# Re-placing the fixed order of sums, splits and hidden work in a seven-product matmul pipeline, and giving the gate and Fourier stage a written order too

## The chip, the cores and the metric

The program runs on one core of a Trainium2 chip. The metric is the time of one execution in device microseconds (us). The engines are TensorE (PE, with its weight loads PEld), VectorE (DVE), ScalarE (ACT), GpSimd (POOL) and SyncE (SP, which here only issues DMAs). Each engine works through its own instructions in order and waits on semaphores for the others.

## The reference

One transformer-like layer for 512 latent and 128 context tokens with 1024 channels, all in 32-bit floats:

```python
h = modulate(rms_norm(x, norm_ffn1), sh1, sc1)
x = x + 0.5 * gt1 * swiglu(h, w_ffn1_gate, w_ffn1_up, w_ffn1_down)
h = modulate(rms_norm(x, norm_mix), sh2, sc2)
y, sf, sb = mixer(h, s_fwd, s_bwd, w_in, ...)
x = x + gt2 * y
h = modulate(rms_norm(x, norm_ffn2), sh3, sc3)
x = x + 0.5 * gt3 * swiglu(h, w_ffn2_gate, w_ffn2_up, w_ffn2_down)
# swiglu(h, wg, wu, wd) = (silu(h @ wg) * (h @ wu)) @ wd, hidden width 2816
# mixer: z = h @ w_in is cut into f, q, k, v, r, a, g;
#   branch_a = Re(fft2 of f in 4 groups of 128 channels) @ w_proj_fourier
#   branch_b = (chunked gated linear attention of q, k, v, a; times silu(r)) @ w_proj_gla
#   y = (sigmoid(g_a) * branch_a + sigmoid(g_b) * branch_b) @ w_out
```

## The kernel before

Activations lie transposed: channels on the 128 partitions, all 640 tokens in the free dimension, in two halves of 320 (`NH`). A 32-bit product is made from two rounded parts, high and low: `split` (lines 107 to 109) lets ACT write the high part and DVE subtract it from the source, and every block of a matmul is three TensorE passes (high by high, high by low, low by high).

Most of the large matmuls go through `Pair7`. It takes two 128-column output blocks at once and treats weights and activations as 2 by 2 blocks, in a scheme with seven products in place of eight. The seven products of a pair are numbered 1 to 7, each 3 passes over up to 4 blocks, 128x320 (12 matmuls for weights of 1024 rows, 9 or 6 for the down matmuls). Each needs one split weight block. Products 7, 5, 6 and 3 need sums of raw weight blocks, made by POOL in place: S3 (line 496) before 7, S1 (492) before 5, S2 (494) before 6, S4 (498) before 3. `STEPS` (line 477) is the order of sums and splits of one pair.

`Pipe.stride` (line 543) writes out the order for one pair `j`, with the products 3 and 4 of the pair before it (`tail3`, `tail4`) put between, and with the weights of the next pair `n` prepared (`ahead`): products 1, 2, 3 of the pair before, 6, 5, 4 of the pair before, 7. The `Take` classes say what is done with the sums in PSUM: `p1`, `p16`, `p167` are ACT copies after products 1, 6 and 7 (lines 606 or 657, 613, 617), on the same bank on which the next product of the chain accumulates, so that product waits for the copy; `p2`, `p53`, `p5` are DVE adds. Two feed-forward stages are made of such pairs: a gate pair (`TakeGate`, silu on ACT), an up pair (`TakeUp`, which multiplies onto the gate, partly on POOL, line 661) and, after each two or three of these, four down pairs. In short: a gate stride (G), an up stride (U), a down stride (D).

What an up pair yields is hidden activation, which is itself the 2 by 2 operand of a down pair: `Hidden7` splits it (line 109 with `pg` as output) and makes its sums, the second half of them on DVE and POOL (lines 719 to 721: two DVE subtractions, one on POOL; line 702 for the first half). In the last part of each feed-forward stage `HiddenPlain` only splits. This work is queued with `pipe.later` and one piece is taken off at each `pend()` of a stride. `halved` (line 368) is the last down matmul of such a stage and `w_out`.

The mixer's second half has the gate projections (`branch_job`, pairs with a sigmoid), the f projection (`tf`) and the Fourier stage (lines 1358 to 1404): for each of four channel groups a fold, channel products (`mm3`, lines 158 to 160), splits, token products. `AdaStream` (from line 922) streams the modulation weights in, 2 MB a step, with 32 small matmuls each (line 215). `pin` (line 57) fixes the order of all instructions since a mark as they were written; what isn't pinned is put in order by a scheduler. Both feed-forward stages and four gate matmuls were pinned, the other gates and the Fourier stage were not.

## Time and profile before

| what | value |
|---|---|
| median of 3 runs | 1634.6 us (1633.91 to 1635.92) |
| the profiled execution, its own time | 1636.21 us |
| span from its first to its last instruction | 1634.2 us |
| PE busy | 1513.0 us (93%), 10994 matmuls |
| PE weight loads busy | 1449.5 us (89%) |
| DVE busy | 1185.5 us (73%) |
| ACT busy | 793.1 us (49%) |
| POOL busy | 597.2 us (37%) |
| mean granted TensorE clock | 0.974 |

The profiled execution is 1.6 us above the median. Engines overlap, so the shares don't add up to one. A busy PE is one with matmuls under way; how fast they follow each other has to be read from their number in a stretch.

### The profile page before, as it was taken

What the parts mean: (1) busy time and instruction counts of PE and PEld (TensorE: products, weight loads), DVE (VectorE), ACT (ScalarE), POOL (GpSimd) and SP (SyncE); (2) the same over time, 40 slices, a digit from 0 to 9 for tenths busy, and PEclk for the clock granted to TensorE, in tenths of its full rate; (3) what the DMA queues carried; (4) which work ended last, traced back from release to release, by engine and by line L of the source; (5) the groups of instructions that cost most, each with busy time, mean ns of one, the idle gap of its engine ahead of it and who ended that gap; (6) DMA issues with size and microseconds to landing.
All of it is one profiled execution on the core that took longest, in us unless ns stands there. A gap on an engine that the chain in (4) does not pass through costs nothing.

```text
span 1634.2 us, 27775 instructions
## 1 busy us (share of the span) xinstructions
PE 1513.0 (93%) x10994; PEld 1449.5 (89%) x10994; DVE 1185.5 (73%) x2001; ACT 793.1 (49%) x1687; POOL 597.2 (37%) x470
## 2 busy tenths in 40 slices
PE   6988989889999999999998998999989988989998
PEld 6988889889999999999898897999989987988997
DVE  6868668768768678486775468687877777866877
ACT  5544444444445546455463354456545444444445
POOL 1444555554530000001343125520445555555540
PEclk8999999999999999999999998999999999999999
DMA  9353222212235421222169216354211221321223
GB/s 359 125 201 136 77 65 91 78 57 73 78 104 167 137 65 39 85 65 75 41 213 398 88 61 236 126 191 136 78 52 59 97 78 41 94 73 65 91 78 117
DMA packets 150425, 183.53 MB, mean 112 GB/s; under 512 B 4799, under 2 KB 124983, under 8 KB 150295
## 3 DMA queue, kind: packets, MB, share of 16 engines
q1 hardware_dynamic: 150295, 181.76, 33.0%
q8 instruction: 86, 1.41, 0.3%
q14 instruction: 44, 0.36, 0.1%
HBM read 167.59 MB, written 14.16 MB: 111 GB/s over the span
## 4 chain that ended last, share of the span: by engine, by line
PE 41%; DVE 29%; POOL 11%; ACT 8%; issue 7%; DMA 4%; SPq 2%; POOLq 0%; ACTq 0%; DVEq 0%
DVE wspl L109 13%; PE pb L516 10%; PE pb L386 6%; PE pb L139 5%; DVE pg L109 5%; PE mm L1035 5%; POOL wraw L496 4%; ACT wspl L108 3%; ACT pg L108 3%; POOL g L661 3%; PE mm L139 2%; DMA pg<-in_w_ada_dram 2%; PE sc L1184 2%; DVE pg L769 2%; DVE hn L664 2%
## 5 line engine op out<-in xcount | busy, mean ns | idle before, releaser
L516 PE MATMUL pb<-pg,wspl 128*128 128x320 f32 x5556 | 867.5, 316 | 72.9 <-ACT hn L657 24.0
L516 PEld LDWEIGHTS pb<-pg,wspl 128*128 128x128 f32 x5556 | 835.5, 192 | 101.7 <-ACT hn L657 27.9
L109 DVE TENSOR_TENSOR wspl<-wraw,wspl 128x512 fp32r<-128x512 f32 (+2 forms) x676 | 550.4, 833 | 206.1 <-ACT wspl L108 203.6
L108 ACT ACTIVATE wspl<-wraw 128x512 fp32r<-128x512 f32 (+2 forms) x676 | 382.0, 589 | 324.3 <-POOL wraw L496 94.6
L496 POOL TENSOR_TENSOR wraw<-wraw 128x512 f32<-128x512 f32 (+2 forms) x74 | 112.7, 1523 | 231.5 <-DVE wspl L109 218.8
L386 PE MATMUL pb<-pg,wspl 128*128 128x320 f32 (+2 forms) x864 | 132.6, 311 | 1.7 <-DVE wspl L109 1.6
L109 DVE TENSOR_TENSOR pg<-g,pg 128x640 fp32r<-128x640 f32 (+1 forms) x90 | 90.5, 1007 | 58.1 <-ACT pg L108 57.8
L386 PEld LDWEIGHTS pb<-pg,wspl 128*128 128x128 f32 x864 | 127.2, 188 | 2.4 <-DVE wspl L109 1.9
L108 ACT ACTIVATE pg<-g 128x640 fp32r<-128x640 f32 (+1 forms) x90 | 61.3, 682 | 125.2 <-DVE g L679 47.3
L139 PE MATMUL pb<-pg,wspl 128*128 128x320 f32 x672 | 106.1, 317 | 7.9 <-DVE pg L1431 7.8
L139 PEld LDWEIGHTS pb<-pg,wspl 128*128 128x128 f32 x672 | 102.1, 193 | 9.3 <-DVE pg L1431 8.5
L494 POOL TENSOR_TENSOR wraw<-wraw 128x512 f32<-128x512 f32 (+2 forms) x74 | 89.8, 1213 | 50.1 <-DVE wspl L109 50.1
L498 POOL TENSOR_TENSOR wraw<-wraw 128x512 f32<-128x512 f32 (+2 forms) x74 | 105.1, 1421 | 5.6
L661 POOL TENSOR_TENSOR g<-g,hn 128x320 f32<-128x320 f32 x48 | 49.5, 1032 | 150.8 <-DVE hn L664 107.7
L492 POOL TENSOR_TENSOR wraw<-wraw 128x512 f32<-128x512 f32 (+2 forms) x74 | 101.9, 1377 | 5.8
L1035 PE MATMUL mm<-wspl,pg 128*128 128x256 f32 x672 | 87.4, 286 | 0.1
L1035 PEld LDWEIGHTS mm<-wspl,pg 128*128 128x128 f32 x672 | 82.4, 191 | 0.5 <-ACT pg L1137 0.3
L1238 POOL TENSOR_TENSOR rs<-ms,negh 128x5 f32<-128x5 f32 x4 | 4.7, 1173 | 205.7 <-DVE ms L1236 205.7
L109 DVE TENSOR_TENSOR pg<-pg,pg 128x320 fp32r<-128x320 f32 (+2 forms) x80 | 57.1, 762 | 9.4 <-ACT pg L108 9.4
L613 ACT ACTIVATE sqh<-pb 128x320 f32<-128x320 f32 x74 | 32.1, 433 | 60.1 <-PE pb L516 60.1
L131 PE MATMUL pb<-pg,wspl 128*128 128x320 f32 x288 | 48.0, 320 | 4.3 <-DVE pg L366 1.9
L139 PE MATMUL mm<-pg,wspl 128*128 128x320 f32 x288 | 51.5, 324 | 0.0
(219 smaller groups left out, 1703.4 us busy)
## 6 DMA issues: line engine op xcount, KB each, us to landing
pg<-in_w_ada_dram SPq DMA_DIRECT2D x72, 512.0 KB, 8.3
wraw<-in_w_ffn_gate_dram SPq DMA_DIRECT2D x22, 1024.0 KB, 4.9
wraw<-in_w_ffn_up_dram SPq DMA_DIRECT2D x22, 1024.0 KB, 5.0
wraw<-in_w_ffn_down_dram SPq DMA_DIRECT2D x28, 768.0 KB, 4.4
wraw<-in_w_in_dram SPq DMA_DIRECT2D x22, 512.0 KB, 3.6
wraw<-in_w_in_dram SPq DMA_DIRECT2D x10, 1024.0 KB, 5.1
wraw<-in_w_out_dram SPq DMA_DIRECT2D x8, 1024.0 KB, 5.1
wraw<-in_w_ffn_down_dram SPq DMA_DIRECT2D x12, 512.0 KB, 3.4
```

The source lines that it names most:

```text
L108: S.activation(out=hi, in_=src, func=AF.Copy)
L109: eng.tensor_tensor(out=lo, in0=src, in1=hi.bitcast(F32), op=ALU.subtract)
L131: T.matmul(out=bank(ps, hf)[:, 0:NH], lhsT=w[a][k], rhs=acts[k][:, b, hf * NH:(hf + 1) * NH], start=(k == 0 and ti == 0), stop=(k == nk - ...
L139: T.matmul(out=bank(ps, hf)[:, 0:NH], lhsT=w[a][k], rhs=acts[k][:, b, hf * NH:(hf + 1) * NH], start=(k == 0 and ti == 0), stop=(k == nk - ...
L386: T.matmul(out=ps[:, 0:c1 - c0], lhsT=w[a][i], rhs=acts[i][:, b, c0:c1], start=(i == 0 and ti == 0), stop=(i == nk - 1 and ti == 2))
L492: G.tensor_tensor(out=self.a21, in0=self.a21, in1=self.a22, op=ALU.add)
L494: G.tensor_tensor(out=self.a11, in0=self.a22, in1=self.a11, op=ALU.subtract)
L496: G.tensor_tensor(out=self.a11, in0=self.a11, in1=self.a21, op=ALU.subtract)
L498: G.tensor_tensor(out=self.a12, in0=self.a12, in1=self.a11, op=ALU.subtract)
L516: T.matmul(out=bank, lhsT=self.w[i][s][k], rhs=x[k][:, t, :], start=first and k == 0 and ti == 0, stop=k == self.n - 1 and ti == 2, skip_g ...
L661: return G.tensor_tensor(out=x, in0=x, in1=part, op=ALU.mult)
L1035: T.matmul(out=ps_out, lhsT=h2[k][:, a, t * P:(t + 1) * P], rhs=w[b][k], start=(k == 0 and ti == 0), stop=(k == KD - 1 and ti == 2))
```

## The change

The order of `STEPS` and the places in `Pipe.stride` are written anew; nothing that is computed changes, and each engine has as many instructions as before.

- The sums of the next pair are made earlier than the splits that read them: S3 before product 6, S1 after it, S2 after product 5 (before: in one go with its split, at the stride's end), S4 at the stride's end (before: in the next stride, ahead of product 2).
- The queue of work (`later`, `pend`) is replaced by named places 1 to 6 in a stride (`at`, `do`). The first split of the hidden activation goes to place 1, the second to 2, its sums to 3, the two splits of sums (mixed, third) to 4, which lies in the next stride behind `p1`. `HiddenPlain` and `TakeY` put their second piece at 3, behind `p5`.
- In the Fourier stage `fold`, `channels`, `between`, `tokens` and `close` become methods, placed by a table (`plan`), and the whole stretch is pinned. `AdaStream` makes one step a stride in eight strides, not two in four.
- `halved` opens six partial sums before it closes the first, not four.

```diff
@@ halved
-                    if hf == 0 and mp < 2:
+                    if hf == 0 and mp < 3:
...
-                if mp == 1:
+                if mp == 2:
@@ Pair7
-        STEPS = (1, 2, "S3", "S1", 7, 5, "S2", 6, "S4", 3, 4)
+        STEPS = (1, 2, "S3", 7, "S1", "S2", 5, 6, "S4", 4, 3)
@@ Pipe.stride
             j.take.p1(j.A)
-            self.pend()
-            j.prep("S4")
+            self.do(4)
+            j.prep(4)
             j.product(2, C, True)
             j.take.p2(C)
             j.prep(3)
-            self.tail3()
-            j.prep(4)
             more()
             ahead(1)
-            mid()
+            self.do(5)
+            self.tail3()
+            ahead("S3")
+            self.do(6)
             j.product(6, j.A, False)
             j.take.p16(j.A)
-            self.pend()
-            ahead("S3")
+            ahead(7)
+            ahead("S1")
             j.B = pb_ps()[:, 0:NH]
             j.product(5, j.B, True)
-            ahead(7)
+            ahead("S2")
+            self.do(1)
             self.tail4()
-            self.pend()
+            self.do(2)
             ahead(5)
             j.product(7, j.A, False)
             j.take.p167(j.A)
             j.take.p5(j.B)
-            self.pend()
-            self.pend()
-            ahead(6)
+            self.do(3)
+            ahead("S4")
@@ Hidden7.second
-            pipe.later(raw, sums, mixed, third)
+            for place, work in ((2, raw), (3, sums), (4, mixed), (4, third)):
+                pipe.at(place, work)
@@ gates and Fourier stage
+    plan = {0: [(2, lambda: dft_split(raws[0])), (3, lambda: dft_split(raws[1]))],
+            1: [(2, lambda: dft_split(raws[2])), (3, lambda: dft_split(raws[3]))],
+            3: [(3, fo[0].fold)],
+            4: [(6, fo[0].channels), (6, fo[0].between), (1, fo[1].fold), (3, fo[0].tokens)],
...
+            7: [(5, fo[3].tokens), (6, fo[3].close)]}
...
+    for i in range(8):
+        for place, work in plan.get(i, ()):
+            pipe.at(place, work)
+        pipe.stride(jobs[0], jobs[1], more)
         jobs.pop(0)
+        stream.step()
+    pin(m2)
@@ TakeY.done
-            pipe.later(work)
+            pipe.at(3 if i else 1, work)
```

The first place is ACT at the end of a gate stride and the start of the up stride behind it, first feed-forward stage (the pairs that the profile shows from 181 us on). `wspl` with `wraw` is a weight split, `pg` with `g` a split of hidden activation, L617 is `p167` of the gate pair, L657 is `p1` of the up pair. Before:

```order
L108 ACTIVATE wspl_2133<-wraw_1950 128x512
L617 ACTIVATE hn_2148<-pb_2021 128x320
L108 ACTIVATE pg_2154<-g_1292 128x640
L108 ACTIVATE wspl_2158<-wraw_1950 128x512
L657 ACTIVATE hn_2175<-pb_2161 128x320
L108 ACTIVATE pg_2177<-g_1291 128x320
L108 ACTIVATE wspl_2194<-wraw_1950 128x512
```

The same place in the change:

```order
L108 ACTIVATE wspl_2134<-wraw_1941 128x512
L617 ACTIVATE hn_2149<-pb_2022 128x320
L108 ACTIVATE wspl_2155<-wraw_1941 128x512
L657 ACTIVATE hn_2173<-pb_2159 128x320
L108 ACTIVATE pg_2175<-g_1310 128x640
L108 ACTIVATE pg_2178<-g_1309 128x320
L108 ACTIVATE wspl_2181<-wraw_1941 128x512
```

The 128x640 split (mixed) stood two rows ahead of `p1` and now stands right behind it; the split for product 6 stays just ahead of `p1`.

The second place is POOL around the same point. L661 and L702 (L707 in the change) end the first half of the hidden activation, L496, L492, L494, L498 are S3, S1, S2, S4 of the next pair, L721 is the hidden sum on POOL. Before:

```order
L702 TENSOR_TENSOR g_1291<-g_1291 128x320
L496 TENSOR_TENSOR wraw_1950<-wraw_1950 128x4x128
L492 TENSOR_TENSOR wraw_1950<-wraw_1950 128x4x128
L721 TENSOR_TENSOR g_1291<-g_1292,g_1291 128x320
L494 TENSOR_TENSOR wraw_1950<-wraw_1950 128x4x128
L498 TENSOR_TENSOR wraw_1950<-wraw_1950 128x4x128
```

In the change:

```order
L707 TENSOR_TENSOR g_1309<-g_1309 128x320
L496 TENSOR_TENSOR wraw_1941<-wraw_1941 128x4x128
L492 TENSOR_TENSOR wraw_1941<-wraw_1941 128x4x128
L494 TENSOR_TENSOR wraw_1941<-wraw_1941 128x4x128
L721 TENSOR_TENSOR g_1309<-g_1310,g_1309 128x320
L498 TENSOR_TENSOR wraw_1941<-wraw_1941 128x4x128
```

S2 has passed the hidden sum; S3 stays behind the end of the first half.

The third place is PE where the Fourier stage begins (lines 158 to 160 are its products, line 215 the modulation's small matmuls, `pb` a PSUM bank). Before:

```order
L215 MATMUL sm_9392<-pg_9256,cs 32x128 x8
L158 MATMUL pb_9489<-pg_8624,pg_9484 128x128
L159 MATMUL pb_9489<-pg_8624,pg_9484 128x128
L158 MATMUL pb_9490<-pg_8624,pg_9484 128x128
L160 MATMUL pb_9489<-pg_8624,pg_9484 128x128
```

In the change:

```order
L516 MATMUL pb_9210<-pg_5420,wspl_9167 128x320 x3
L158 MATMUL pb_9380<-pg_8709,pg_9266 128x128
L159 MATMUL pb_9380<-pg_8709,pg_9266 128x128
L160 MATMUL pb_9380<-pg_8709,pg_9266 128x128
L158 MATMUL pb_9380<-pg_8730,pg_9266 128x128
```

The channel products came behind two steps of the modulation; they now stand inside a stride, between products 3 and 6, a stride after their fold was issued.

## Rows read from the trace of the kernel before

**Rows 1.** Groups by line, PE: busy us, mean ns | idle us before, and releasers.

```profile
L516 PE MATMUL pb<-pg,wspl 128*128 128x320 f32 x5556 | 867.5, 316 | 72.9 <-ACT hn L657 24.0 <-DVE wspl L109 14.7 <-DVE g L620 11.4
L386 PE MATMUL pb<-pg,wspl 128*128 128x320 f32 (+2 forms) x864 | 132.6, 311 | 1.7 <-DVE wspl L109 1.6
```

**Rows 2.** Windows: length, busy PE, PEld, DVE, ACT, POOL (instructions), clock, DMA share, GB/s.

```profile
90.14:478.43 388.29, 357.98 (x2504) 345.10 (x2501) 288.48 (x452) 181.39 (x371) 205.39 (x163) 0.97 0.28 91
834.62:994.16 159.54, 149.05 (x1367) 140.94 (x1365) 97.92 (x171) 72.65 (x151) 46.20 (x32) 0.97 0.55 198
994.16:1030.11 35.95, 28.15 (x170) 27.49 (x169) 29.72 (x46) 13.84 (x28) 16.80 (x14) 0.86 0.59 204
1030.11:1087.02 56.91, 52.82 (x357) 51.94 (x355) 43.67 (x58) 25.05 (x47) 31.57 (x24) 1.00 0.39 129
1191.17:1588.61 397.44, 364.22 (x2330) 351.81 (x2329) 295.43 (x446) 187.94 (x379) 213.56 (x165) 0.97 0.23 73
179.07:209.38 30.31, 26.96 (x170) 26.18 (x169) 20.88 (x28) 14.23 (x27) 16.86 (x14) 0.94 0.22 71
```

**Rows 3.** Timeline of PE in feed-forward 1: start, length, matmuls, wait before.

```profile
163.82 18.94 PE L516 MATMUL pb<-pg,wspl 128*128 128x320 f32 x128
183.42 2.02 PE L516 MATMUL pb<-pg,wspl 128*128 128x320 f32 x12 [0.66 <-DVE g L620]
187.30 0.56 PE L516 MATMUL pb<-pg,wspl 128*128 128x320 f32 x2 [1.86 <-ACT hn L657]
188.68 24.38 PE L516 MATMUL pb<-pg,wspl 128*128 128x320 f32 x154 [0.82 <-DVE wspl L109]
```

**Rows 4.** Timeline of ACT: end of the gate stride, start of the up stride.

```profile
184.33 0.74 ACT L108 ACTIVATE pg<-g 128x640 fp32r<-128x640 f32 x1 [1.98 <-DVE g L720]
186.29 0.63 ACT L108 ACTIVATE wspl<-wraw 128x512 fp32r<-128x512 f32 x1 [1.23 <-POOL wraw L494]
186.83 0.42 ACT L657 ACTIVATE hn<-pb 128x320 f32<-128x320 f32 x1
```

**Rows 5.** Timeline of DVE from 175 us.

```profile
177.95 2.39 DVE L109 TENSOR_TENSOR wspl<-wraw,wspl 128x512 fp32r<-128x512 f32 x2
...
181.54 0.82 DVE L109 TENSOR_TENSOR pg<-g,pg 128x640 fp32r<-128x640 f32 x1 [0.80 <-ACT pg L108]
182.28 0.69 DVE L109 TENSOR_TENSOR wspl<-wraw,wspl 128x512 fp32r<-128x512 f32 x1
182.88 0.48 DVE L620 TENSOR_TENSOR g<-hn,pb 128x320 f32<-128x320 f32 x1
...
185.10 1.85 DVE L109 TENSOR_TENSOR pg<-g,pg 128x640 fp32r<-128x640 f32 x1 [0.80 <-ACT pg L108]
```

**Rows 6.** Timeline of POOL from 175 us.

```profile
176.05 1.30 POOL L496 TENSOR_TENSOR wraw<-wraw 128x512 f32<-128x512 f32 x1
177.42 1.76 POOL L492 TENSOR_TENSOR wraw<-wraw 128x512 f32<-128x512 f32 x1
183.91 1.12 POOL L721 TENSOR_TENSOR g<-g,g 128x320 f32<-128x320 f32 x1 [4.73 <-DVE g L719]
184.99 1.27 POOL L494 TENSOR_TENSOR wraw<-wraw 128x512 f32<-128x512 f32 x1
...
191.27 0.87 POOL L661 TENSOR_TENSOR g<-g,hn 128x320 f32<-128x320 f32 x1 [3.20 <-ACT g L643]
```

**Rows 7.** Waits of PE, whole program: total us, times, longest.

```profile
PE pb L516 <- ACT hn L657: 24.0, 15, 1.9
...
PE pb L516 <- ACT hn L606: 5.8, 7, 1.9
```

**Rows 8.** Waits of PE in the window of gates and Fourier stage.

```profile
PE pb L516 <- ACT hn L617: 4.2, 4, 2.7
PE pb L160 <- DVE pg L109: 3.0, 1, 3.0
```

**Rows 9.** Waits of PE in the window of w_proj_gla.

```profile
PE pb L516 <- DVE hn L664: 4.0, 2, 2.8
```

More of the change, by code (lines that the diff above doesn't have):

```diff
@@ L707, in first @@
             self.x0 = x0
-            pipe.later(work)
+            G.tensor_tensor(out=x0[:, NH:N], in0=x0[:, NH:N], in1=x0[:, 0:NH], op=ALU.subtract)
+            pipe.at(1, work)
         def second(self, x1):
@@ L744, in work, with first, second @@
                 self.append(h)
-            pipe.later(work)
-        second = first
+            pipe.at(place, work)
+        def first(self, x):
+            self.put(x, 1)
+        def second(self, x):
+            self.put(x, 3)
     class TakeUp(TakeMul):
@@ L1321, in trunk_kernel, with dft_load, dft_split @@
     act.each(act.put1)
-    pin(m2)
-    stream = AdaStream((5, 7, 6, 8))
-    def two_steps():
-        stream.step()
-        stream.step()
-    dft, four = [], []
-    for j in range(4):
+    dft, four, mT = [], [], []
+    def dft_load(j):
         raw = page()
         SP.dma_start(out=raw[:, 0, :], in_=I["k_dft"][j * P:(j + 1) * P, :])
+        return raw
+    def dft_split(raw):
         t = page(F32R)
@@ new lines, in trunk_kernel, with __init__, fold, channels @@
+    class Fourier:
+        def __init__(self, mp):
+            self.mp = mp
+        def fold(self):
+            f = (tf[self.mp // 2].x0, tf[self.mp // 2].x1)[self.mp % 2]
+            eo = page()[:, 0, 0:512]
+            fe, fo = eo[:, 0:256], eo[:, 256:512]
+            V.tensor_copy(fe[:, 0:1], f[:, 0:1])
+            V.tensor_tensor(out=fe[:, 1:256], in0=f[:, 1:256], in1=f[:, 511:256:-1], op=ALU.add)
+            V.memset(fo[:, 0:1], 0.0)
+            V.tensor_tensor(out=fo[:, 1:256], in0=f[:, 1:256], in1=f[:, 511:256:-1], op=ALU.subtract)
+            fn = sm_tile([P, P], "junk")
+            V.memset(fn, 0.0)
+            V.tensor_copy(fn[:, 0:1], f[:, 256:257])
+            self.nyq = sm_tile([P, 2, P], "junk", F32R)
+            split(self.nyq[:, 0, :], self.nyq[:, 1, :], fn)
+            self.ehl = page(F32R)
+            split(self.ehl[:, 0, 0:512], self.ehl[:, 1, 0:512], eo)
+            split(self.ehl[:, 0, 512:N], self.ehl[:, 1, 512:N], f[:, NL:N])
+        def channels(self):
+            ehl, nyq = self.ehl, self.nyq
+            cc, ss = four[0], four[1]
+            self.ua, self.ub = ua, ub = pb_ps(), pb_ps()
+            for j in range(2):
+                mm3(ua[:, j * P:(j + 1) * P], [ehl[:, i, j * P:(j + 1) * P] for i in range(2)], cc)
+                mm3(ua[:, (2 + j) * P:(3 + j) * P], [ehl[:, i, (2 + j) * P:(3 + j) * P] for i in range(2)], ss,
+                    stop=(j == 1))
+                if j == 0:
+                    mm3(ua[:, 2 * P:3 * P], [nyq[:, i, :] for i in range(2)], cc, start=False)
+            xc = [ehl[:, i, 512:N] for i in range(2)]
+            mm3(ub[:, 0:P], xc, cc)
+            mm3(ub[:, P:2 * P], xc, ss)
+        def between(self):
+            self.us = page(F32R)
+            self.us2 = sm_tile([P, 2, P], "junk", F32R)
+            split(self.us[:, 0, 0:512], self.us[:, 1, 0:512], self.ua)
+            split(self.us[:, 0, 512:N], self.us[:, 1, 512:N], self.ub[:, 0:P])
+            split(self.us2[:, 0, :], self.us2[:, 1, :], self.ub[:, P:2 * P])
+        def tokens(self):
+            us, us2 = self.us, self.us2
+            c1, s1 = four[2], four[3]
+            self.ya, self.yb = ya, yb = pb_ps(), pb_ps()
@@ L1398, in token_part, with close, more @@
             mm3(yb[:, 0:P], [us2[:, i, :] for i in range(2)], s1, start=False)
+        def close(self):
             m = page(F32R)
[L1400 to L1401 removed]
+            split(m[:, 0, 0:NL], m[:, 1, 0:NL], self.ya)
+            split(m[:, 0, NL:N], m[:, 1, NL:N], self.yb[:, 0:NC])
             mT.append(m)
[L1404 removed]
+    fo = [Fourier(mp) for mp in range(4)]
+    raws = [dft_load(j) for j in range(4)]
+    todo = [lambda g=g: Pair7(load(w_in, 0, KD, C_F + g * 256, 256), act, tf[g]) for g in range(2)]
+    todo += [lambda mp=mp: branch_job(0, mp) for mp in range(4)]
+    jobs = [one, two]
+    plan = {0: [(2, lambda: dft_split(raws[0])), (3, lambda: dft_split(raws[1]))],
+            1: [(2, lambda: dft_split(raws[2])), (3, lambda: dft_split(raws[3]))],
+            3: [(3, fo[0].fold)],
+            4: [(6, fo[0].channels), (6, fo[0].between), (1, fo[1].fold), (3, fo[0].tokens)],
+            5: [(4, fo[0].close), (5, fo[1].channels), (5, fo[1].between), (1, fo[1].tokens), (2, fo[2].fold),
+                (3, fo[1].close)],
+            6: [(4, fo[2].channels), (4, fo[2].between), (6, fo[3].fold), (1, fo[2].tokens), (2, fo[2].close),
+                (3, fo[3].channels), (3, fo[3].between)],
+            7: [(5, fo[3].tokens), (6, fo[3].close)]}
+    def more():
+        jobs.append(todo.pop(0)() if todo else None)
+    for i in range(8):
+        for place, work in plan.get(i, ()):
+            pipe.at(place, work)
+        pipe.stride(jobs[0], jobs[1], more)
         jobs.pop(0)
+        stream.step()
+    pin(m2)
     yap = [page() for _ in range(4)]
@@ L1460, in work @@
                 split(y[:, 0, :], y[:, 1, :], x)
-            pipe.later(work)
+            pipe.at(3 if i else 1, work)
     act.each(act.put4)
```

78 lines of the change are left out of this document (15 added, 63 removed).

## The prediction, made before the changed kernel ran

> **What bounds the kernel now.** I looked first at the windows of the stretches [rows 2]: PE is busy in 358 of 388 us in the first feed-forward stage, 364 of 397 in the second, 149 of 160 in gates and Fourier stage. So TensorE is the bound, and all that an order can win is what it loses to waits and to its clock. When nothing holds it, 128 matmuls take 18.94 us [rows 3]; less the 0.32 us of the last one, that is 0.147 us each, 1.76 us for a product of 12. A gate and an up stride are 168 matmuls, 24.7 us; the period in the last window of [rows 2] takes 30.31. The 5.6 us between are three waits of 0.66, 1.86 and 0.82 us [rows 3] (a wait is listed only from the end of the last matmul, so each costs some 0.15 more: 3.8 in all) and the clock: granted 0.94 there, so about 1.8 us lost at the lower level of 1.2 GHz. Over the stretches the granted clock of 0.97 costs 0.03 x 388 = 11.6 us, 0.03 x 397 = 11.9 us and 0.03 x 160 = 4.8 us [rows 2].
>
> Where the waits come from is read next, in the timelines of ACT, DVE and POOL around 183 us. ACT goes through its list: the mixed split waits 1.98 us for a DVE sum, the weight split for product 6 waits 1.23 us for S2 on POOL, and only then `p1` (L657) copies the bank at 186.83 [rows 4]; product 6 starts at 187.30 [rows 3]. Fifteen waits in the program are of this kind, after a gate stride with folded hidden work behind it; seven are the same at the start of a gate stride (L606), 5.8 us in all or 0.8 each [rows 7]. All pair products together wait 72.9 us [rows 1].
>
> There is a second limit beneath. The DVE half of a split takes 0.69 us at 182.28, but two of them 2.39 us at 177.95 [rows 5], while POOL makes S1 until 179.18 [rows 6]. The 640-wide one takes 0.82 us alone and 1.85 at 185.10 [rows 5], beside S2, which ends at 186.26 [rows 6]: it ends 0.69 us after POOL. So DVE instructions with two SBUF inputs and POOL's take turns, with some 0.13 us of overlap at a turn. A period has, on POOL, 8 sums at 1.27, 3 multiplications at 0.87, 2 hidden sums at 1.12 [rows 6] = 15.0 us, and on DVE 14 splits at 0.69, 3 at 0.82 and three 320-wide at 0.48 (the time of `p5`, the nearest row) [rows 5] = 13.6. That is 28.6 us in turns; with some 20 overlaps of 0.13, 26.0. PE's 24.7 lies below both.
>
> The Trainium skill, "SBUF — State Buffer", section "SBUF: two separate sides", says that a VectorE instruction with two SBUF inputs and a GpSimd instruction hold a shared pair of ports exclusively, whoever starts first, for the whole instruction. The rows agree but for the 0.13 us. It speaks against this change: a sum moved beside a split wins nothing on that pair; by the rule a period stays at 28.6 at the least.
>
> **The change, part by part.** *Feed-forward order.* S2 passes the hidden sum on POOL and the mixed split goes behind `p1`, so both things that held `p1` are gone. What is late next I follow by hand from the start of a gate stride, products 1.76 us apart, with these durations and turns. DVE's add of product 3 ends at 6.7; POOL follows with a multiplication, a subtraction and S3, to 10.4 (in the trace S3 ends at 177.35 [rows 6], 10.6 after the start of that stride). The split for product 7 now stands alone behind S3 and holds ACT from 7.7 to 10.4; behind it queue the first hidden split, the raw one, the split for 5 and `p167`, so `p5` ends at 16.5. In the trace it ended 16.6 after the start (183.36 [rows 5]): this lateness stays, and product 3, due at 15.8, waits 0.7. DVE then does two sums, and its half of the split for 6 waits for POOL's hidden sum: 19.0, where product 6 is due at 18.3, again 0.7. Behind that, mixed, third, 4, `p2`, 3, 1 and the gate's add fill DVE to 24.4; ACT's silu, a split and `p16` end at 26.2, where product 7 is due at 24.3: 1.9. In all 3.3 us; the next period starts about 1 us behind and comes to 4.2. In a down stride product 6 itself reads the mixed split, some 2.7 late; with the first wait about 3.8. I take 3.7 for each of the 15, against 4.1 now (3.8 and small drains): 15 x 0.4 = 6 us. The seven waits at a gate stride's start go, since S2 is two products old there: 7 x 0.95 with the drain, 6 us. Of the 72.9 us, 24.0 and 5.8 are these two kinds, 15 x (0.66 + 0.82) = 22 the other two waits of the fifteen strides, 8 lie in the later stages [rows 8, 9]; some 13 are left, smaller ones in first strides, behind down strides and in the parts with plain hidden splits, whose second split now stands behind `p5`: I take 10. Together 22.
>
> The clock: the waits that stay are single. One of 2.8 us in the pairs of w_proj_gla [rows 9] left the clock at 1.00 there [rows 2], while the bunch of three within 6 us brought 0.94. I take two thirds of 23.5 as won: 16. Feed-forward stages: **-38 us**. The ends are 0 (every wait only moves, the clock too) and -80 (periods at 26.0, the down and first strides likewise, clock at 1.00). I stand nearer the middle since the hand-followed queue gives 28.0 and 28.8 for a period.
>
> *Gates and Fourier stage.* PE is not busy for 10.5 us [rows 2], of which 4.2 and 3.0 are the waits of [rows 8]; with the clock's 4.8 that is 15. The 3.0 is a Fourier product whose split had not been made; in the written order the channel products stand three products (5.3 us) behind their fold, whose dozen small DVE instructions and splits I put at 4 us from the rows of splits, and the token products two or more behind `between`. One modulation step a stride spreads 2 MB over some 18 us, with the DMA share at 0.55 [rows 2]; the k_dft loads, now ahead on SP's queue, and pages held for longer are covered by that. I leave 4 us of new waits: **-11 us**. Ends: -15 and +8 (four groups, each 2 us late, a split and a fold behind a product).
>
> *w_proj_gla.* `TakeY`'s second split moves behind `p5`, the add that product 3 waits for, 4.0 us in two waits [rows 9]: **-3.5**, ends 0 and -4.
>
> *The rest.* `halved` with six open sums gains at most the 1.6 us that its matmuls wait for a split [rows 1], and may lose two splits' time, 2.6 us, as six blocks of nine are held: 0. The end of the Fourier stage, where 35.95 us hold 168 matmuls and a clock of 0.86 [rows 2], has the same code behind it: 0, ends -5 and +5 by when its pages come free. The fold's buffer moved to a page, and `out` moved from `p1` to `p2`: nothing, they issue no work.
>
> Sum: -38 - 11 - 3.5 = -52.5. The profiled execution took 1636.2 us, so **1584 us** (that execution stands 1.6 above the median of the runs, which I leave in the rounding).
>
> **Rivals.** *It comes out at the pair of engines' floor.* DVE and POOL never idle, and periods come to 26.0: feed-forward -80, gates -14, w_proj_gla -4: 1538 us. For it: DVE is busy 20.9 of 30.3 us in the period [rows 2], so it has idle time to give. Against it: the chain from product 3's add over POOL to S3 and ACT is as it was. By the skill's rule above this rival can't be; it would stop at 28.6, a period's gain of 1.7, near my own numbers. Chance 0.12.
>
> *The waits only move.* The fifteen strides lose as much as now and the clock drops as often; only the gate strides' waits, half of the small ones and half of the gates' are won: -6 -5 -6 = 1619 us, or nothing at all. Chance 0.14, of it 0.06 within 0.2% (3.3 us, about what a measurement of this kernel can tell from no change).
>
> *Slower: mixed and third ahead of everything.* They now stand at the head of the next stride on ACT and DVE, before the splits for 4, 3, 1, 2 and `p16`. If POOL takes its turn before each of them, L721 (1.12) and S4 (1.27) [rows 6] come on top of my 3.7: 15 x (3.7 + 2.4 - 4.1) = +30, the clock stays, 16 are won elsewhere in the feed-forward stages and 3 in the rest: +11, 1647 us. It decides from some 6 us lost in an up or down stride behind a gate stride. For it: in my own ledger product 7 is already 1.9 late. Against it: product 7 has two products between, and DVE idles before. Chance 0.13.
>
> That the change doesn't do what it says is excluded on the engines' lists: S2 stands ahead of L721 and mixed behind `p1`.
>
> **How the numbers follow.** My forecast has 0.61, with its own range of 1560 to 1610. To hold eight in ten I reach to part of both neighbours: 1550 to 1628. Faster by over 0.2%: 0.61 + 0.12 + 0.08 = 0.81; within: 0.06; slower: 0.13.
>
> **What would show it.** Right: no PE wait on L657 and L606 worth the name; the period near 28 to 29 us with waits on `p5`, on a split before product 6, and a new one on L613 (`p16`) before product 7; clock at 0.99 in the feed-forward stages; L160 without its 3 us; no wait of 2.8 us in w_proj_gla. Wrong: periods at 26 (then my queue is too slow by hand), or up strides that lose 6 us before products 6 and 7, or Fourier products that wait on their splits.

## The result and the profile after

The changed kernel takes 1564.6 us (median of 4 runs, 1563.12 to 1568.54). The kernel before takes 1635.3 (4 runs, 1633.91 to 1636.32). The ratio is 0.957, 95% interval 0.955 to 0.959. The forecast was 1584 us with a range of 1550 to 1628, so sign and range hold, and 71 us were gained where 52.5 were expected. The profiled execution took 1564.67 us, its span is 1562.9 us.

Where the time came from, by the starts of PE's matmuls (each stretch has the same matmuls in both kernels):

| stretch | before | after | difference | forecast |
|---|---|---|---|---|
| up to the first pair of feed-forward 1 | 90.1 | 88.7 | -1.5 | 0 |
| feed-forward 1 and 2 | 785.7 | 732.8 | -52.9 | -38 |
| halved, norm, projections, attention | 356.2 | 358.9 | +2.7 | 0 |
| gates and Fourier stage | 159.5 | 141.9 | -17.6 | -11 |
| end of the Fourier stage | 36.0 | 29.9 | -6.0 | 0 |
| w_proj_gla | 56.9 | 58.0 | +1.1 | -3.5 |
| w_out and what follows, to feed-forward 2 | 104.2 | 104.2 | 0 | 0 |
| last halved and output | 45.6 | 48.5 | +2.9 | 0 |
| span | 1634.2 | 1562.9 | -71.3 | -52.5 |

The windows of the changed kernel that answer to [rows 2] (length; busy PE, PEld, DVE, ACT, POOL with instructions; clock, DMA share, GB/s), in the table's order from feed-forward 1 on, and last one period of an up and a gate stride:

```profile
88.67:451.35 362.68, 344.61 (x2504) 336.08 (x2501) 291.98 (x454) 181.10 (x373) 200.17 (x163) 1.00 0.30 99
810.25:952.16 141.91, 141.91 (x1366) 136.80 (x1365) 88.31 (x174) 70.43 (x153) 42.93 (x32) 1.00 0.65 223
952.16:982.10 29.94, 27.10 (x170) 25.97 (x169) 26.90 (x43) 12.43 (x25) 15.59 (x13) 0.94 0.62 199
982.10:1040.07 57.97, 53.93 (x356) 53.40 (x355) 44.06 (x58) 25.27 (x47) 31.21 (x24) 0.97 0.43 140
1144.29:1514.42 370.13, 351.26 (x2331) 344.25 (x2329) 300.12 (x448) 186.12 (x378) 207.46 (x165) 0.99 0.25 79
1514.42:1562.90 48.48, 38.09 (x258) 35.68 (x256) 33.19 (x90) 23.64 (x102) 3.32 (x4) 0.96 0.31 109
172.88:201.46 28.58, 25.34 (x171) 24.65 (x170) 20.66 (x27) 14.28 (x28) 17.83 (x14) 1.00 0.23 74
```

The clock of the feed-forward stages went from 0.97 to 1.00 and 0.99. In the gate and Fourier stage PE is busy in all of its 141.91 us. The period is 28.58 us instead of 30.31 and has no lower clock.

The group of the pair products on the page, which answers to [rows 1], and PE's waits in the whole program (total us, times, longest), which answer to [rows 7 to 9]:

```profile
L516 PE MATMUL pb<-pg,wspl 128*128 128x320 f32 x5556 | 839.7, 311 | 42.2 <-DVE g L620 15.1
```

```profile
PE pb L516 <- DVE g L620: 15.1, 15, 3.5
PE pb L516 <- ACT sqh L613: 12.4, 14, 1.2
PE pb L516 <- DVE hn L664: 6.7, 5, 2.8
PE pb L516 <- DVE pg L109: 6.0, 11, 0.9
...
PE pb L139 <- DVE pg L1460: 2.7, 2, 2.0
```

The copies L657 (24.0 us before) and L606 (5.8) are no longer among them, nor is L160. The copy p16 (L613) holds PE for 12.4 us where it held it for 1.1 in two waits before. Idle time before pair products fell from 72.9 to 42.2 us.

PE's timeline in the stretch that answers to [rows 3] (start, length, matmuls, wait before):

```profile
178.61 7.47 PE L516 MATMUL pb<-pg,wspl 128*128 128x320 f32 x48 [2.05 <-DVE g L620]
187.28 17.86 PE L516 MATMUL pb<-pg,wspl 128*128 128x320 f32 x120 [1.20 <-ACT sqh L613]
206.68 7.46 PE L516 MATMUL pb<-pg,wspl 128*128 128x320 f32 x48 [1.54 <-DVE g L620]
215.35 4.96 PE L516 MATMUL pb<-pg,wspl 128*128 128x320 f32 x32 [1.21 <-ACT sqh L613]
```

Product 3 of the pair before waits for p5, and 48 matmuls (four products) later product 7 waits for p16. Product 6, which lost most before, has no listed wait in the up strides. In the down strides it still waits some 0.57 us for the mixed split (part of the 6.0 us on L109 above). The second of these strides starts at 201.46, its gate stride at 189.13. POOL, ACT and DVE there, one fence each:

```profile
197.47 1.25 POOL L661 TENSOR_TENSOR g<-g,sqh 128x320 f32<-128x320 f32 x1 [2.47 <-DVE sqh L664]
198.80 0.88 POOL L707 TENSOR_TENSOR g<-g 128x320 f32<-128x320 f32 x1
199.64 1.30 POOL L496 TENSOR_TENSOR wraw<-wraw 128x512 f32<-128x512 f32 x1
...
207.17 1.12 POOL L721 TENSOR_TENSOR g<-g,g 128x320 f32<-128x320 f32 x1 [2.42 <-DVE g L719]
```

```profile
195.03 1.68 ACT L108 ACTIVATE wspl<-wraw 128x512 fp32r<-128x512 f32 x3 [2.50 <-POOL wraw L498]
...
200.97 0.63 ACT L108 ACTIVATE wspl<-wraw 128x512 fp32r<-128x512 f32 x1 [3.95 <-POOL wraw L496]
201.51 0.72 ACT L108 ACTIVATE pg<-g 128x640 fp32r<-128x640 f32 x1
204.03 0.74 ACT L108 ACTIVATE pg<-g 128x640 fp32r<-128x640 f32 x1 [1.80 <-DVE g L679]
...
205.19 0.42 ACT L617 ACTIVATE hn<-pb 128x320 f32<-128x320 f32 x1
...
213.71 0.74 ACT L643 ACTIVATE g<-g 128x640 f32<-128x640 f32 x1 [2.53 <-DVE g L642]
...
214.88 0.42 ACT L613 ACTIVATE sqh<-pb 128x320 f32<-128x320 f32 x1
```

```profile
196.91 0.48 DVE L664 TENSOR_TENSOR sqh<-sqh,pb 128x320 f32<-128x320 f32 x1
...
203.51 0.48 DVE L679 TENSOR_TENSOR g<-pb,g 128x320 f32<-128x320 f32 x1
...
206.14 0.48 DVE L620 TENSOR_TENSOR g<-hn,pb 128x320 f32<-128x320 f32 x1
...
207.47 1.37 DVE L109 TENSOR_TENSOR wspl<-wraw,wspl 128x512 fp32r<-128x512 f32 x1
```

S3 (L496) starts only at 199.64, behind two POOL pieces that wait for DVE's add of the product 3 before (L664, 196.91). ACT stands 3.95 us for S3, then 1.80 us for L679, and copies p167 at 205.19. So p5 (L620) ends at 206.62, and product 3 was due at 204.98. This is the chain that the prediction followed by hand. Behind it the DVE half of the split for product 6 (207.47) stands beside POOL's hidden sum (L721). Later ACT waits 2.53 us for DVE before the gate's silu (L643), and the copy p16 stands behind that.

### The profile page after: what moved, and what is told of

Read it like the earlier page. It is cut to its first block, busy times and chain, and to the rows that moved or that the text cites. A ratio compares the mean times of both kernels' runs of the same rounds, so it can differ in the third digit from the quotient of the medians.

```text
span 1562.9 us, 27799 instructions
## 1 busy us (share of the span) xinstructions
PE 1481.5 (95%) x10994; PEld 1429.8 (91%) x10994; DVE 1175.6 (75%) x2001; ACT 785.7 (50%) x1687; POOL 582.2 (37%) x470
## 4 chain that ended last, share of the span: by engine, by line
PE 47%; DVE 30%; POOL 10%; ACT 5%; issue 5%; DMA 2%; POOLq 0%; SPq 0%; ACTq 0%; DVEq 0%
PE pb L516 16%; DVE wspl L109 13%; PE pb L139 6%; PE pb L386 5%; PE mm L1040 5%; DVE pg L774 5%; DVE pg L109 4%; POOL g L661 3%; ACT wspl L108 3%; PE mm L139 2%; POOL wraw L496 2%; PE sc L1189 2%; DVE hn L664 2%; POOL wraw L498 2%; PE sm L215 2%
## 5 line engine op out<-in xcount | busy, mean ns | idle before, releaser
L516 PE MATMUL pb<-pg,wspl 128*128 128x320 f32 x5556 | 839.7, 311 | 42.2 <-DVE g L620 15.1
L516 PEld LDWEIGHTS pb<-pg,wspl 128*128 128x128 f32 x5556 | 819.7, 189 | 59.4 <-DVE g L620 19.3
L109 DVE TENSOR_TENSOR wspl<-wraw,wspl 128x512 fp32r<-128x512 f32 (+2 forms) x676 | 513.3, 780 | 197.2 <-ACT wspl L108 195.3
L496 POOL TENSOR_TENSOR wraw<-wraw 128x512 f32<-128x512 f32 (+2 forms) x74 | 89.8, 1214 | 241.2 <-DVE wspl L109 227.7
L494 POOL TENSOR_TENSOR wraw<-wraw 128x512 f32<-128x512 f32 (+2 forms) x74 | 104.1, 1407 | 102.0 <-DVE wspl L109 102.0
L386 PEld LDWEIGHTS pb<-pg,wspl 128*128 128x128 f32 x864 | 127.2, 188 | 2.1 <-DVE wspl L109 1.9
L498 POOL TENSOR_TENSOR wraw<-wraw 128x512 f32<-128x512 f32 (+2 forms) x74 | 110.0, 1486 | 3.1
L139 PE MATMUL pb<-pg,wspl 128*128 128x320 f32 x672 | 105.2, 315 | 3.0 <-DVE pg L1460 2.7
L139 PEld LDWEIGHTS pb<-pg,wspl 128*128 128x128 f32 x672 | 100.5, 190 | 5.1 <-DVE pg L1460 4.0
L492 POOL TENSOR_TENSOR wraw<-wraw 128x512 f32<-128x512 f32 (+2 forms) x74 | 96.4, 1303 | 4.2
L109 DVE TENSOR_TENSOR pg<-g,pg 128x640 fp32r<-128x640 f32 x86 | 85.1, 1006 | 16.0 <-ACT pg L108 16.0
L108 ACT ACTIVATE pg<-g 128x640 fp32r<-128x640 f32 x86 | 58.4, 682 | 63.8 <-DVE g L679 26.0
L661 POOL TENSOR_TENSOR g<-g,hn 128x320 f32<-128x320 f32 x48 | 53.2, 1109 | 62.8 <-DVE hn L664 51.3
L109 DVE TENSOR_TENSOR pg<-pg,pg 128x320 fp32r<-128x320 f32 (+2 forms) x84 | 57.3, 729 | 11.9 <-ACT pg L108 11.7
L613 ACT ACTIVATE sqh<-pb 128x320 f32<-128x320 f32 x74 | 31.8, 430 | 54.1 <-PE pb L516 54.1
L617 ACT ACTIVATE hn<-pb 128x320 f32<-128x320 f32 x74 | 31.8, 430 | 41.4 <-PE pb L516 41.4
L131 PE MATMUL pb<-pg,wspl 128*128 128x320 f32 x288 | 48.0, 321 | 3.9 <-DVE pg L366 1.9
```

The lines of the kernel that those rows point to most:

```text
L108: S.activation(out=hi, in_=src, func=AF.Copy)
L109: eng.tensor_tensor(out=lo, in0=src, in1=hi.bitcast(F32), op=ALU.subtract)
L139: T.matmul(out=bank(ps, hf)[:, 0:NH], lhsT=w[a][k], rhs=acts[k][:, b, hf * NH:(hf + 1) * NH], start=(k == 0 and ti == 0), stop=(k == nk - ...
L386: T.matmul(out=ps[:, 0:c1 - c0], lhsT=w[a][i], rhs=acts[i][:, b, c0:c1], start=(i == 0 and ti == 0), stop=(i == nk - 1 and ti == 2))
L492: G.tensor_tensor(out=self.a21, in0=self.a21, in1=self.a22, op=ALU.add)
L494: G.tensor_tensor(out=self.a11, in0=self.a22, in1=self.a11, op=ALU.subtract)
```

## The experiments

The runs ask three things: which part of the change carries which gain, what holds the strides now, and whether that can be taken away. Each expectation sets a theory against a rival, and behind the measured time stands which of the two it bears out. "Feed-forward sum" is the two stages as in the table, from each kernel's one trace. The traced execution stands 4.5 us above the median of its runs with S2 late, 5.3 with S2 alone and 3.0 with place 1 behind product 4, and within 2.4 us of it otherwise, so a difference of 2 or 3 us between two sums shows little.

**S2 late.** One part undone:

```diff
-        STEPS = (1, 2, "S3", 7, "S1", "S2", 5, 6, "S4", 4, 3)
+        STEPS = (1, 2, "S3", 7, "S1", 5, "S2", 6, "S4", 4, 3)
...
-            ahead("S2")
```

> The changed kernel with one part undone: S2 is made again at the stride's end, behind the hidden sum on POOL, together with the split for product 6. Theory (S2 ahead of the hidden sum is what frees p1): in the trace of the change the hidden sum on POOL ends 1.6 us after product 3 of the gate pair has begun, S2 would end at about +2.9, its split at +3.5, p1 at +4; product 6 is due at +1.8, so each of the fifteen strides loses 2 to 2.7 us more and each of the seven gate strides 1.4 (what they lost before); with the clock some +40 to +55, 1605 to 1620 us, and L657 and L606 are back among PE's waits. Rival (only the 1.23 us that the split waited for S2 come back, the rest of the gain is the other parts'): +18 to +25, 1583 to 1590 us.

1601.7 us, ratio 0.9775 (0.9751 to 0.9799) where the change has 0.957. The feed-forward sum is 765.6. PE's timeline there:

```profile
183.60 2.03 PE L516 MATMUL pb<-pg,wspl 128*128 128x320 f32 x12 [1.32 <-DVE g L619]
187.47 0.56 PE L516 MATMUL pb<-pg,wspl 128*128 128x320 f32 x2 [1.85 <-ACT hn L656]
188.38 24.38 PE L516 MATMUL pb<-pg,wspl 128*128 128x320 f32 x154 [0.35 <-DVE wspl L109]
```

The p1 wait (L656 here) is back with 1.85 us, 25.2 us in 15 waits, as long as before [rows 3, 7]. So 33 of the 53 us hang on S2 by the traces; by the medians of the runs its undoing costs 37 us. The time lies between the rival's range and the theory's, nearer to the theory. Of the gate strides' waits (L606 before, L604 here) 3.0 us in three came back, of 5.8 in seven, which is less than the theory counted.

**Mixed ahead of p1 again.**

```diff
-            for place, work in ((2, raw), (3, sums), (4, mixed), (4, third)):
+            for place, work in ((2, raw), (3, sums), (3, mixed), (4, third)):
```

> The changed kernel with one part undone: the mixed split of the hidden activation goes back to the end of the stride, ahead of the split for product 6 and of p1 (the third split stays behind p1). Theory (each of the two things that held p1 costs by itself): mixed waits on ACT for DVE's second sum, p1 ends about 2.8 us later than in the change, product 6 is due 0.9 us before that and its split is late too: +1 to +1.7 us in each of fifteen strides, 15 to 25 in all, 1580 to 1590 us, with waits on L657. Rival (p5 is late anyway, and product 6 comes behind product 3, so that mixed is covered): within 5 us of the change, 1560 to 1570.

1569.9 us, ratio 0.9584 (0.9564 to 0.9604), feed-forward sum 736.8: the time is in the rival's range. PE:

```profile
184.51 0.56 PE L516 MATMUL pb<-pg,wspl 128*128 128x320 f32 x2 [0.52 <-ACT hn L657]
186.15 26.14 PE L516 MATMUL pb<-pg,wspl 128*128 128x320 f32 x166 [1.08 <-DVE wspl L109]
```

With mixed in front, p1 costs 0.52 us and the split behind it 1.08, but p16 is then on time, and the wait before product 7 is absent. Mixed's move is worth 4 us in the feed-forward stages, and by the traces it is all the clock: the two stages have 18.2 us at the lower clock here and 6.8 in the change, which at half speed is 5.7 us. Without the clock the strides lose no more than in the change.

**Both undone.** The two edits above together.

> S2 late and mixed ahead of p1, both as before the change; S3, S1, the hidden work's other places and the Fourier stage as in the change. Theory (the feed-forward gain of 53 us is these two moves): 1610 to 1622 us, feed-forward stages within 6 us of the time before in sum, clock again near 0.97 there. Rival (the two are not additive, or the earlier places of S1, S3 and of the split for 4 carry a good part): 1590 to 1605.

1603.5 us, ratio 0.9792 (0.9764 to 0.9821), feed-forward sum 767.8: the time is in the rival's range. With S2 late it makes no difference where mixed stands (765.6 and 767.8).

**S2 alone**, put into the kernel before:

```diff
-        STEPS = (1, 2, "S3", "S1", 7, 5, "S2", 6, "S4", 3, 4)
+        STEPS = (1, 2, "S3", "S1", 7, "S2", 5, 6, "S4", 3, 4)
...
             ahead(7)
+            ahead("S2")
             self.tail4()
```

> The kernel before with one part of the change alone: S2 is made behind product 5, right behind S1, so that it passes the hidden sum on POOL; mixed, the queue, S3, S4 and the Fourier stage stay as they were. Theory (S2's place carries most of the feed-forward gain, mixed almost none): the two kernels that differ in S2 alone while mixed is in its old place measured 1603.5 and 1569.9 us, so the same 33.6 us come off the time before: 1597 to 1607 us, L657 with waits of 0.5 us instead of 1.9. Rival (in the old order mixed and the queue hold p1 as long as S2 does, and S2 alone wins nothing much): 1620 to 1635.

1618.8 us, ratio 0.9899 (0.9872 to 0.9926), feed-forward sum 767.1. That is 18.6 us less than before. The time lies between theory and rival, just below the rival's range; the theory's 33.6 fails. PE:

```profile
211.19 2.02 PE L516 MATMUL pb<-pg,wspl 128*128 128x320 f32 x12 [1.75 <-DVE g L621]
213.73 0.56 PE L516 MATMUL pb<-pg,wspl 128*128 128x320 f32 x2 [0.52 <-ACT hn L658]
215.38 23.57 PE L516 MATMUL pb<-pg,wspl 128*128 128x320 f32 x148 [1.09 <-DVE wspl L109]
```

p1 is down to 0.52 as expected; but three waits are left here, and the small ones behind down strides stay too. The sums of the four kernels read together: S2 alone takes 18.6 us off, the rest without S2 20.1, both 52.9. The parts help each other by some 14 us. The medians of the runs agree: S2 alone takes 17.4 us off the whole program, all but S2 37.4, everything 70.7, which is 16 more than the two together. The two stages' time at the lower clock shows one way: 45.2 us before, 23.9 with S2 alone, 34.1 with the rest alone, 6.8 with both; at half speed that is 22.6, 12.0, 17.1 and 3.4 us lost, so 3.1 of the 14 us are the clock's and the rest is in waits.

**The gate and Fourier stage as it was**, in the new stride order (the stage's old code, its token products at place 6).

> The changed kernel with the gate and Fourier stage as it was: four strides with two modulation steps each, then four groups in a loop, left to the scheduler; the new stride order stays. Theory (the written order is what took the 17.6 us out of that stage, and the 6.0 us of the Fourier end with it): +20 to +25, 1585 to 1590 us, a wait on L160 of some 3 us back. Rival 1 (the pairs' new order carries half of it, as S2 no longer holds p1 there either): +8 to +13, 1573 to 1578. Rival 2 (the Fourier end's 6 us come with the new order of the sums, not with the stage): the end stays at 30 us and the stage alone returns to about 155.

1588.5 us, ratio 0.9695 (0.9674 to 0.9716): the theory holds. Windows of the stage and of its end:

```profile
811.99:969.44 157.45, 147.68 (x1366) 139.63 (x1365) 97.38 (x171) 72.38 (x151) 46.12 (x32) 0.98 0.56 202
969.44:1005.49 36.05, 28.04 (x171) 27.37 (x169) 30.14 (x46) 13.95 (x28) 17.04 (x14) 0.86 0.57 195
```

So 15.5 of the stage's 17.6 us come with its new code and 2.1 with the new strides. The new code is the order, the pin and one modulation step a stride; no run parts these. The end's 6 us come with it as well: 36.05 with the old code here, 27.7 to 32.4 in every kernel with the new one. The wait on L160 is back with 3.2 us in two, and L617 with 3.4 in four.

**Halved with four open sums.**

```diff
-                    if hf == 0 and mp < 3:
+                    if hf == 0 and mp < 2:
...
-                if mp == 2:
+                if mp == 1:
```

> The changed kernel with halved as it was, four sums open instead of six. Theory (closing six sums in a row bunches the residual adds, transposes and norm copies at the program's end, which lost 2.9 us against before): -1.5 to -3 us, 1561.5 to 1563 us, and the PE wait of 1.2 us for L393 gone. Rival (the end is late because its last weights land late, now that the stage before is shorter: ACT waits 0.7, 1.7 and 0.3 us for w_ffn_down there): within 0.7 us.

1565.5 us, ratio 0.9558 (0.9532 to 0.9584): the times don't tell the two apart. Its last stretch does in part:

```profile
1516.76:1563.10 46.34, 37.80 (x258) 35.84 (x256) 32.48 (x90) 22.94 (x101) 3.31 (x4) 0.95 0.31 114
```

46.3 us against 48.5, and PE's wait for L393 is 0.5 us in two there, 1.7 in three in the change. The other traces point the same way: this stretch takes 45.3 to 46.3 us in the three kernels with four open sums and 46.8 to 50.5 in the eleven with six. So six open sums probably cost about 2 us at the end.

**w_proj_gla pinned** in the written order.

```diff
     act.each(act.put4)
+    m4 = mark()
     pipe.chain([lambda mp=mp: Pair7(load(I["w_proj_gla"], 0, KD, mp * 256, 256), act, TakeY(mp)) for mp in range(4)])
+    pin(m4)
```

> The changed kernel with the pairs of w_proj_gla pinned in the written order. In the trace of the change the second split of TakeY still stands ahead of the copy p167 and of p5 on ACT and DVE, because the scheduler orders this stretch. Theory (in the written place the split is behind p5 and product 3 no longer waits): the two waits of 2.8 and 1.25 us on L664 go, with drains and clock 4 to 6 us, 1558 to 1561 us. Rival (pinned, the next stage's first splits and loads lose the gaps the scheduler gave them): 0 to +4.

1573.5 us, ratio 0.9608 (0.9583 to 0.9632): slower by more than the rival said. PE in a middle stride, with the split now behind p5:

```profile
1015.11 2.02 PE L516 MATMUL pb<-pg,wspl 128*128 128x320 f32 x12 [1.93 <-DVE hn L664]
1017.47 0.57 PE L516 MATMUL pb<-pg,wspl 128*128 128x320 f32 x2 [0.33 <-ACT hn L657]
1019.11 10.53 PE L516 MATMUL pb<-pg,wspl 128*128 128x320 f32 x70 [1.08 <-DVE wspl L109]
```

p5 is late all the same (1.93 us), and the split behind it delays product 6. In the first stride, products wait 1.04 and 1.28 us for weight splits that the scheduler had drawn ahead. The waits on p5 (L664) fell only from 4.0 to 3.3 us. So moving TakeY's split did not free p5, and what holds p5 there stays open.

**S3 first.** Now what is left. One line moved:

```diff
             self.do(5)
+            ahead("S3")
             self.tail3()
-            ahead("S3")
```

> The changed kernel with one move more: S3 of the next pair is issued ahead of product 3 of the pair before, so that POOL makes it before the gate multiplication and the hidden subtraction that wait for that product, not behind them. Theory (the wait on p5 that is left in the up strides comes from the chain product 3, POOL's two pieces, S3, split for 7, first hidden split, raw split, p167, p5): in the period from 189 us S3 would begin at about 197.0 instead of 199.64, L679 comes 1.3 us earlier, and the waits of 1.5 to 2.0 us on L620 shrink to 0 to 0.7; 11 to 17 us off the feed-forward stages, 1548 to 1554 us. Rival (VectorE and GpSimd take turns, so what POOL does earlier DVE does later): under 4 us, 1561 to 1566. The Trainium skill, page SBUF — State Buffer, section SBUF: two separate sides, gives the second, and no gate-and-up period below 28.6 us in the mean.

1549.3 us, ratio 0.9462 (0.9432 to 0.9493), feed-forward sum 718.4: the theory holds. POOL around the same stride (its gate stride starts at 187.24):

```profile
195.04 1.68 POOL L496 TENSOR_TENSOR wraw<-wraw 128x512 f32<-128x512 f32 x1 [2.07 <-DVE wspl L109]
196.68 0.87 POOL L661 TENSOR_TENSOR g<-g,sqh 128x320 f32<-128x320 f32 x1
```

S3 begins 7.8 us into the gate stride instead of 10.5 (199.64 - 189.13), and the two waits on p5 are 1.01 and 0.62 us instead of 2.05 and 1.54. Three periods of this kernel:

```profile
171.94:199.56 27.62, 25.32 (x170) 24.63 (x169) 18.45 (x27) 14.29 (x28) 18.54 (x14) 1.00 0.23 77
290.74:316.35 25.61, 24.91 (x171) 24.64 (x169) 16.90 (x25) 13.86 (x27) 16.55 (x13) 1.00 0.25 83
316.35:343.58 27.23, 25.33 (x170) 24.63 (x169) 18.75 (x28) 13.75 (x28) 18.29 (x15) 1.00 0.18 59
```

All three are below the 28.6 us that the prediction gave DVE and POOL in strict turns; in sum they hold 80 DVE and 42 POOL instructions, where three times the period of [rows 2] would be 84 and 42. The section on the hardware comes back to this.

**The silu late.** The silu of the gate's first half goes behind p16. In this kernel it also stands behind the up pair's first multiplication, which so reads that half without its silu; time and order are what it is for.

```diff
             self.last = V.tensor_tensor(out=self.x0[:, NH:N], in0=self.w, in1=ps, op=ALU.add)
+
+        def act0(self):
             S.activation(out=self.x0, in_=self.x0, func=self.func)
             self.done(0)
...
             j.take.p16(j.A)
+            if self.prev:
+                self.prev.take.act0()
```

> The changed kernel with one move more: the silu (or sigmoid) of a gate's first half, which ACT does behind product 3's add, is issued behind the copy after product 6 (p16), not ahead of it. Theory (product 7 waits for p16 since ACT stands 2.5 us behind the DVE queue for that silu): the 12.4 us of waits on L613 go, with their drains 10 to 14 us, 1551 to 1555 us. Rival (ACT is late there because the splits before it are, the copy ends no earlier, or p5 of the same stride waits instead): within 4 us of the change, 1561 to 1568.

1564.4 us, ratio 0.9553 (0.9528 to 0.9579): the rival holds. PE:

```profile
179.69 12.75 PE L516 MATMUL pb<-pg,wspl 128*128 128x320 f32 x84 [0.51 <-DVE g L627]
193.43 12.58 PE L516 MATMUL pb<-pg,wspl 128*128 128x320 f32 x84 [0.99 <-DVE hn L673]
208.10 12.75 PE L516 MATMUL pb<-pg,wspl 128*128 128x320 f32 x84 [2.10 <-DVE g L627]
```

The wait on p16 is gone; product 3 waits for p5 in the up strides as before and now in the gate strides too (L673). The queue behind sets the time.

**S3 first and p16 first**, with the silu between p16 and the multiplication. The cut shows the stride alone; the silu is parted from the add as in the run above, and the multiplication from the copy:

```diff
             j.take.p16(j.A)
+            if self.prev:
+                self.prev.take.act0()
+            j.take.onto16()
```

> The change with S3 ahead of product 3 of the pair before, and the copy p16 on ACT ahead of the silu of the gate's first half, which stands ahead of the up pair's first multiplication. Theory (p16 late is a wait of its own): the 11.7 us of waits on L613 go and at most a third of them comes back as a wait on p5, 1539 to 1545 us. Rival (the engines' queues behind are late by the same amount, and product 3 of the next stride waits instead, as in the kernel with the silu late, whose time didn't change): 1547 to 1552.

1542.0 us, ratio 0.9424 (0.9403 to 0.9444), feed-forward sum 713.6: the time is in the theory's range. L613 is gone from the waits; L620's line has 10.5 us against 8.0 with S3 first alone, L664's 9.0 against 5.9. Of 11.7 us, 5.6 came back so, half and not a third. With the queue shortened, p16 is worth something.

**S3 first, and place 1 behind product 4.**

```diff
-            self.do(1)
             self.tail4()
+            self.do(1)
             self.do(2)
```

> The change with S3 ahead of product 3 of the pair before, and the first hidden split behind product 4 and its multiplication, not ahead of them. Theory (the 0.8 to 1.2 us that product 3 still waits for p5 come from VectorE doing the first hidden split, which waits for POOL, ahead of the multiplication behind product 4): the 8.0 us of waits on L620 fall under 3, 1541 to 1546 us. Rival (the raw split then waits behind the first one, and p167 as late as before): 1547 to 1552.

1547.9 us, ratio 0.9452 (0.9422 to 0.9481): the total is in the rival's range. The feed-forward sum fell to 713.3, though (L620 5.2 us), and the gate and Fourier stage, whose folds stand at place 1 as well, grew by 3.3 us. Hence the last run: S3 first and p16 first as above, and only the hidden activation's first split at place 2 (the cut shows what is added to that kernel).

```diff
-            pipe.at(1, work)
+            pipe.at(2, work)
```

> The kernel with S3 ahead of product 3 and p16 ahead of the silu (1542.0 us), and only the first hidden split moved behind product 4 and its multiplication; the Fourier stage's pieces stay where they are (moving all of place 1 cost the gate and Fourier stage 3.3 us). Theory (the wait of 1.2 us behind product 2 of the five down strides comes from that split's place, and a part of the up strides' wait for p5): 5 x 1.2 and 8 x 0.4 = 9 us, half of it given back behind, 1534 to 1539 us, gate and Fourier stage at 134.7. Rival (the strides are at what DVE and POOL can do between them, and the wait turns up in the gate strides or before product 6): 1541 to 1544.

**1537.4 us**, ratio 0.939 (0.9359 to 0.9421), feed-forward sum 709.0: the time is in the theory's range, and this is the fastest kernel here, 27 us below the change. The gate and Fourier stage takes 141.9 us as in the change, not the 134.7 that was expected. Its waits and the period that answers to 172.88:

```profile
PE pb L516 <- DVE g L631: 9.3, 11, 2.6
PE pb L516 <- DVE hn L677: 8.6, 9, 2.8
...
PE pb L516 <- DVE pg L109: 3.5, 6, 0.6
```

```profile
172.67:199.39 26.72, 25.32 (x170) 24.63 (x169) 19.60 (x27) 13.74 (x27) 17.86 (x14) 1.00 0.25 80
```

## Why the prediction was right, and where its numbers were off

*What moved.* The mechanism was right: L657 and L606 are gone, p5 holds product 3, p16 holds product 7, and the period is 28.6 us where 28.0 and 28.8 were followed by hand. The split for product 6 also went as followed: its DVE half runs beside POOL's hidden sum and ends at 208.84. But the matmul that reads it first starts only 0.17 us late, too little to be listed, since the wait for p5 had already put product 6 back.

The sizes were off. By the starts of the matmuls, eight of the nine up strides lose 0.8 to 2.3 us before product 3, 0.2 before 6 and 1.5 before 7, where I had 0.7, 0.7 and 1.9. So the period came out right in part by luck, since these errors set each other off. The first of them has a cause in the rows: I took over from the trace before that DVE's add of product 3 ends 6.7 us after the start of the gate stride. In the change it ends at 8.3 (196.91 + 0.48 - 189.13), because ACT stands 2.50 us for S4 (L498) ahead of it and DVE has that split's half to do first; S3 then ends at 11.8 where I had 10.4. In the down strides product 6 loses 0.9 us, where I had the mixed split 2.7 late.

*The fifteen strides.* Forecast 15 x 0.4 = 6 us. With a free product at 1.76 us, and half of the time at the lower clock taken off, the strides lost 52.0 us before and 46.4 after: 5.6. The difference was right, though both levels were not: 3.5 and 3.1 us a stride where I had 4.1 and 3.7.

*The other strides.* Here is most of the miss. I counted 6 us for seven gate strides (7 x 0.95 is 6.7) and 10 for the small waits, 16 in all. By the same measure all strides but the fifteen lost 33.0 us before and 4.8 after: 28. Those seven gate strides lost 1.4 us each or more, 13.5 in all, and lose 2.0 now, since with L606 went the wait on the split behind it and the short gaps around both; and of the small ones nearly all went, not ten of thirteen. A list of waits, from which I summed, leaves out the gaps too short to be listed.

*The clock.* Forecast 16 of 23.5 us, measured 22.6 - 3.4 = 19. The direction was right for the reason given: in feed-forward 1 single waits of 1.2 to 2.05 us, several us apart, left it at 1.00. What is left, 6.8 us at the lower clock, lies in feed-forward 2 around the one wait of 3.5 us (L620).

*S2 and mixed as a pair.* "Both things that held p1 are gone" treated them as equals. S2 is the one that counts (33 us to undo it, 4 for mixed, and these through the clock). In the timeline before, mixed's wait stood ahead of S2's on ACT [rows 4], yet S2 was late by itself.

*Gates and Fourier stage.* Forecast -11, ends -15 and +8; -17.6 came, beyond the end. The 15 was summed from idle PE and clock alone. PE's busy time fell by 7.1 us as well (149.05 to 141.91), of which the clock's 4.8 are a part; the other 2 lay in gaps too short to count as idle. And the 4 us of new waits that I left did not come: PE never stops there.

*The Fourier end.* Forecast 0, "the same code behind it". The same code met other queues: the wait of its products on L1431, 6.4 us before, is 2.0 (L1460). The run with the old stage shows that it hangs on the stage's code (36.05). Why is read from the traces alone and not shown by a run: S3 of the next pair starts 0.9 us into the stretch, 4.1 before and 4.4 with the old stage, and PE's wait for DVE's add ends 9.3 us into it, against 13.6 and 13.8.

*w_proj_gla.* This step failed: "`TakeY`'s second split moves behind `p5`". The source moves it; on the engines the scheduler, which orders this stretch, left it ahead of p167 and p5. The order of the engines' lists shows this, and I read the diff for this part only. Pinned, it won nothing either. The 1.1 us lost are clock (below).

*The rest.* +2.7 us in the middle is probably not the change's. The kernel with S2 alone, with the code of before there, took 359.4 in that stretch, and every trace but the one before 358.2 to 361.4. Of the +2.9 at the end some 2 us are probably the six open sums that I put at 0.

*Rivals.* "The waits only move" did not hold, but is seen in the silu run. "Mixed and third ahead of everything" did not either: up strides lose 3.1 us, not 6. "The floor of DVE and POOL" at 26.0 was not reached by the change, but the S3 run comes to 25.6 to 27.6.

## What to carry to other kernels

When an in-order engine copies the bank that the next product needs, look for the latest thing queued ahead of it and move that thing's producer, not the copy; then look at what is latest next: here S2, then S3, then p16, each by a small edit. By the rows, S4 may be next; that was not run. Moving a waiting piece that isn't the latest (mixed, or the silu while S3 was late) bought 4 us or nothing here, and the gains of two moves need not add. Take moves from the engines' lists, not from the source, wherever a scheduler has the last word, and sum what a stretch loses from the starts of its matmuls rather than from a list of waits.
